# A state-space stage cut into short steps between projection blocks, with half of one map and the table loads moved to GpSimd

## The chip, the cores and the metric

The kernel runs on one core of one Trainium2 chip. The metric is the device time of one execution in microseconds (us), the median of the runs shown. Matrix products run on TensorE (PE, its weight loads PEld), elementwise work on VectorE (DVE), ScalarE (ACT) and GpSimd (POOL). SyncE (SP) issues DMAs; GpSimd can issue them too. Each engine takes its instructions in order, and a wait on one holds everything behind it on that engine.

## The reference

Two layers on a sequence of 512 tokens with 1024 channels, in float32; each is `x <- x + RMSNorm_post(mixer(RMSNorm_pre(x)))`. The change touches layer 0, whose mixer has two branches:

```
p = u @ ev_w_in[j]                       # 1024 -> 5120
a_in, a_z, b_val, b_gate, b_z = split(p)
ya = s5_layer(a_in, ...)                 # 64 groups of 16 channels, 64 complex states each
ya = gelu(ya)
ya = ya * sigmoid(ya @ s5_w_glu + s5_b_glu) * silu(a_z)
yb = conformer_conv(b_val, b_gate, ...)  # GLU, depthwise conv of 31 taps, LayerNorm, swish, projection
y  = concatenate([ya, yb * silu(b_z)]) @ ev_w_out
```

The state-space layer computes `s_t = Lbar s_(t-1) + Bbar u_t` and `y_t = Re(C s_t) + D u_t` per group. Layer 1 is a gated linear attention, which the change leaves as it is.

## The kernel before, in words

**Projections.** Every float32 product is made of three passes: a weight is split into a high part `wh` and a low part `wl` (float32r), the activation into `uh` and `ul`, and `mm_st` (L181) adds `wh uh`, `wh ul` (L186, L187) and `wl uh` (L189) into one PSUM bank. One block is 24 such matmuls on 512 columns and makes 128 output channels. Layer 0 has 40 input blocks: eight `a` blocks (the state-space input), and eight each of value `v`, gate `g`, `zb` and `za`. `wlist` (L85 to L94) holds the order of their weights: all `a` first, then v, g, zb, za for each j.

**Weights.** `w_raw` (L113) loads a block's 512 KB by SyncE's queue into `wraw`, which has three buffers. `w_low` (L122) makes the low part: ScalarE writes the negated rounding (L130), and a DMA that GpSimd issues adds the raw weights to it (L131). ScalarE also makes `wh` (L143). A raw buffer is free when all this has read it. `w_get` keeps one block split ahead.

**The state-space stage** works on eight chunks of eight groups. `s5_params` (L308) computes tables on VectorE and GpSimd: powers `pr` (nine of them, real and imaginary) and `prb`, and the phase tables' factors `wb`. `s5_prep(c)` (L513) loads a chunk's B and C matrices `cb` by SyncE's queue (L519); makes `cr_` (C's real part with a sign per half, L522) and `ci_` (its negated imaginary part, L523) on ScalarE; and, per half of four groups: the input map `bmt`, three products with `outer` (L528, L530, L532) on VectorE for the first two chunks and on GpSimd after; its transposes (L544) into `bm`; the response (L551), copied to `ks` (L554), transposed (L555), and written to `kt` (L557); the output map `cme`, three products on VectorE. Then `kt` goes through DRAM into the Toeplitz matrix `tm` (L563, L565). For every other chunk `phases` (L492) builds two tables `ph0`, `ph1` on GpSimd in six products, which four DMAs on SyncE's queue duplicate into `ct` and `st` (L573). `s5_in` (L579) loads `u` back from DRAM (L584), applies `bm` (L588), turns the result (L595), rotates, scans and rotates back on VectorE and ScalarE. `s5_out` (L619) applies `tm` and `cme` (L628) and transposes to channels with a GELU (L637, L643).

**The convolution** (`conv`, L649): 30 VectorE multiply-adds of 745 ns for each of eight channel blocks (L655, L656), marked `background`.

**What sets the order.** The generators `s5_prep`, `s5_in` and `s5_out` yield between their steps, and a loop (L703) writes the steps of chunks c, c+1 and c+2, then four blocks. This written order is a priority. The scheduler that builds the program places each engine's instructions by priority among those that its own timing says are ready; `feed()` raises a priority by 1500 places and `background()` lowers it by 4000. A pool opened with `reuse_waits="tile"` waits for the earlier owners of its bytes tile by tile.

Of the kernel before, what the change touches and what calls it, by code (L numbers as in the profile page):

```python
# [51 lines left out]
def trunk(ctx: ExitStack, tc: tile.TileContext, A: dict, out: bass.AP, dbg: dict | None = None):  # L52
# [33 lines left out]
    for j in range(8):  # L86
        wlist.append(A["w_in0"][j])
    for j in range(8):
        wlist.append(A["w_in0"][16 + j])
        wlist.append(A["w_in0"][24 + j])  # L90
        wlist.append(A["w_in0"][32 + j])
        wlist.append(A["w_in0"][8 + j])
# [20 lines left out]
    def w_raw():  # L113
        i = wst["next_raw"]
        if i >= len(wlist):
            return
        raw = wpool.tile([P, 1024], F32, tag="wraw", bufs=3, name=f"wraw{i}")
        SY.dma_start(raw, wlist[i])
        wst["raw"][i] = raw
        wst["next_raw"] = i + 1  # L120
# [187 lines left out]
    def s5_params():  # L308
# [148 lines left out]

        G.memset(md, 0.0)
# [6 lines left out]
    q5 = S5.enter_context(tc.tile_pool(name="q5", bufs=1, side="right", reuse_waits="tile"))  # L465
    h5 = S5.enter_context(tc.tile_pool(name="h5", bufs=2, side="right", reuse_waits="tile"))
# [25 lines left out]
    def phases(c):  # L492
# [10 lines left out]
        out_ = []  # L503
        for o, (a, b, op) in enumerate(((0, 1, ALU.subtract), (1, 0, ALU.add))):
            r_ = h5.tile(sh, F32, tag=f"ph{o}", bufs=1, name=f"ph{o}_{c}")
            wt = h5.tile(sh, F32, tag="wt", bufs=1, name=f"wt{o}_{c}")
            G.tensor_tensor(out=r_, in0=w1(0), in1=w0(a), op=ALU.mult)
            G.tensor_tensor(out=wt, in0=w1(1), in1=w0(b), op=ALU.mult)
            G.tensor_tensor(out=r_, in0=r_, in1=wt, op=op)
            out_.append(r_.rearrange("p g a b -> p (g a b)"))  # L510
        pair[c // 2] = out_

    def s5_prep(c):  # L513
# [3 lines left out]
        gs = slice(g0_, g0_ + GC)  # L517
        cb = h5.tile([P, 4, GC, GP], F32, tag="cb", bufs=2, name=f"cb{c}")
        SY.dma_start(cb, A["s5cb"][c])  # L519
# [3 lines left out]
        SC.mul(ci_, cb[:, 1], -1.0)  # L523
# [10 lines left out]
        bm = q5.tile([P, GC, P], F32, tag="bm", bufs=2, name=f"bm{c}")  # L534
        cme = q5.tile([P, GC, TB, GP], F32, tag="cme", bufs=3, name=f"cme{c}")
        kt = q5.tile([P, GC, GP], F32, tag="kt", bufs=2, name=f"kt{c}")
        for h in range(2):
            hs = slice(h * 4, h * 4 + 4)
            bmt = q5.tile([P, 4, GP, TB], F32, tag="bmt", bufs=2, name=f"bmt{c}")
            pt1 = h5.tile([P, 4, GP, TB], F32, tag="wt", bufs=1, name=f"pt1_{c}")  # L540
            outer(pe_, bmt, pt1, h, prb, cb[:, 2, hs], cb[:, 3, hs], 2)
            tp = ps("aux")
            for j in range(4):
                PE.transpose(tp[:, j * P:(j + 1) * P], bmt[:, j].rearrange("p q s -> p (q s)"), ident)  # L544
            with feed():
                SC.copy(bm[:, hs, :], tp.rearrange("p (g n) -> p g n", n=P))
            yield

            kp = ps("aux")
            for j in range(4):  # L550
                PE.matmul(kp[32 * j:32 * j + 32, 0:P], cr_[:, h * 4 + j, :], bmt[:, j].rearrange("p q s -> p (q s)"), start=True, stop=True)  # L551
# [3 lines left out]
            PE.transpose(kp[:, P:2 * P], ks, ident)  # L555
            with feed():
                V.tensor_tensor(out=kt[:, hs, :], in0=kp[:, P:2 * P].rearrange("p (g q) -> p g q", q=32)[:, :, 0:GP],  # L557
                                in1=dg[:, g0_ + h * 4:g0_ + h * 4 + 4, :], op=ALU.add)
            pt2 = q5.tile([P, 4, TB, GP], F32, tag="pt", bufs=1, name=f"pt2_{c}")
            outer(V, cme[:, hs], pt2, h, pr, cr_[:, hs, 0:GP], ci_[:, hs], 3)  # L560
            yield
# [4 lines left out]

        if c % 2 == 0:
            phases(c)
        half = slice(c % 2 * NS, c % 2 * NS + NS)
        ct_, st_ = (h5.tile([P, S], F32, tag=n, bufs=2, name=f"{n}{c}") for n in ("ct", "st"))  # L570
        for dst, src in zip((ct_, st_), pair[c // 2]):
            for r_ in range(2):
                SY.dma_start(dst[r_ * NS:r_ * NS + NS], src[half])  # L573
        prep[c] = (bm, cme, tm, ct_, st_)
        yield

    state = {}

    def s5_in(c):  # L579

        g0_ = c * GC
        bm, cme, tm, cc, ss = prep.pop(c)
        u = h5.tile([P, GC, NB], F32, tag="u", name=f"u{c}")
        SY.dma_start(u, bass.AP(tensor=u_d[c].tensor, offset=u_d[c].offset, ap=[[NB, P], [S * GP, GC], [1, NB]]))  # L584
        gp = ps("aux")
# [73 lines left out]
    for c in range(KT):  # L659
# [3 lines left out]
        with feed():  # L663
            ai = tmp((P, TB, NB))
            SC.copy(ai, acc.rearrange("p (b s) -> p s b", s=TB))
            SY.dma_start(u_d[c], ai)

    def value_gate(c):
        w = w_get()
        av = ps()  # L670
        mm_st(av, w, uh, ul)
        w = w_get()
        ag = ps()
        mm_st(ag, w, uh, ul)
        h = hpool.tile([P, 30 + S], F32, tag="h", name=f"h{c}")
        G.memset(h[:, 0:30], 0.0)
        with feed():
            sg = tmp()
            SC.activation(sg, ag, AF.Sigmoid)  # L679
            V.tensor_mul(h[:, 30:30 + S], av, sg)  # L680
        htile[c] = h
        with background():
# [534 lines left out]
```

## Time and profile before

| | |
|---|---|
| median of 3 runs | 944.95 us (944.75 to 949.93) |
| the profiled execution | 946.38 us, span 944.7 us |
| mean granted TensorE clock | 0.981 |
| ScalarE, VectorE, GpSimd busy | 485.1, 641.9, 245.4 us |
| HBM read, written | 95.18 MB, 13.22 MB |
| low-part DMAs (L131) | 56, median 6.1 us from issue to landing |
| input weight loads | 40, median 5.2 us from issue to landing |

A row of waits names the instruction that waited, after the arrow what released it, then the total, the number of times and the longest, in us. A row of a timeline gives the start, the duration, the engine, the line, the operation and its shape, and in brackets the idle time before it with what ended it. A row of grouped lines gives count, busy time, mean ns of one, and the idle time before. A row of windows gives the stretch, its length, each engine's busy time (PE, PEld, DVE, ACT, POOL; with an engine filter that engine alone), the granted clock, the DMA engines' mean busy share, and GB/s. SPq rows are DMA issues; their duration includes SyncE's wait before them. Matmuls overlap, so one's duration is longer than the distance between two starts.

### The profile page before, as it was taken

The numbers are of one execution on the slowest core, as the hardware profiler recorded it, in microseconds if no ns is written. First come the engines' busy times: TensorE is split into PE (matmuls) and PEld (weight loads), VectorE is DVE, ScalarE is ACT, GpSimd is POOL, SyncE is SP. The second block draws the span as 40 slices with busy tenths as digits, with TensorE's granted clock in tenths as the row PEclk, the third lists the DMA queues.
The fourth block names the chain that finished last, engine by engine and source line by source line (L and its number), as shares of the span: only waits on it lengthen the run. The fifth ranks groups of instructions, "written<-read, shape, count | busy, mean of one in ns | idle before, by whom it ended". The sixth has DMA issues, their size and how long they took to land. (4 is left out here: it accounts for less than half of the span.)

```text
span 944.7 us, 12134 instructions
## 1 busy us (share of the span) xinstructions
PE 897.7 (95%) x4396; PEld 718.9 (76%) x4396; DVE 641.9 (68%) x1206; ACT 485.1 (51%) x693; POOL 245.4 (26%) x258
## 2 busy tenths in 40 slices
PE   5995998999999999999999979999999999999996
PEld 4873776777778877778887758888888888888875
DVE  7953999999989989832579477584483232744546
ACT  6542786786678855564444566343543242523430
POOL 2693657463123422011054002000200020000222
PEclk8998999999999999999999979999999999999998
DMA  9877987787988885288463112212212223324412
GB/s 278 228 198 194 229 199 184 178 205 204 215 220 228 210 231 179 92 224 201 153 215 124 45 63 93 84 37 82 90 67 90 73 83 135 134 89 164 193 45 89
DMA packets 54955, 142.74 MB, mean 151 GB/s; under 512 B 14256, under 2 KB 15792, under 8 KB 54896
## 3 DMA queue, kind: packets, MB, share of 16 engines
q1 hardware_dynamic: 46832, 112.62, 35.9%
q0 software_dynamic: 8064, 29.36, 17.3%
q8 instruction: 34, 0.56, 0.2%
q14 instruction: 25, 0.20, 0.1%
HBM read 95.18 MB, written 13.22 MB: 115 GB/s over the span
## 5 line engine op out<-in xcount | busy, mean ns | idle before, releaser
L143 ACT CAST wh<-wraw 128x1024 fp32r<-128x1024 f32 x126 | 132.1, 1048 | 161.4 <-PE ps_mm L801 92.5
L149 DVE TENSOR_TENSOR wl<-wraw,wh 128x1024 fp32r<-128x1024 f32 x70 | 87.0, 1243 | 115.2 <-ACT wh L143 114.8
L655 DVE SCALAR_TENSOR_TENSOR ps_cv<-h,cw,ps_cv 128x512 f32<-128x512 f32 x232 | 161.7, 745 | 2.7 <-ACT ps_cv L652 1.8
L186 PE MATMUL ps_mm<-u0h,wh 128*128 128x512 f32 x320 | 129.9, 407 | 1.0 <-ACT tmp L679 0.7
L187 PE MATMUL ps_mm<-u0l,wh 128*128 128x512 f32 x320 | 129.4, 405 | 0.0
L800 PE MATMUL ps_mm<-wh,u1h 128*128 128x512 f32 x240 | 96.2, 402 | 3.5 <-ACT wh L143 3.4
L801 PE MATMUL ps_mm<-wh,u1l 128*128 128x512 f32 x240 | 96.3, 401 | 0.8 <-DVE u1l L194 0.8
L131 POOL DMA_DIRECT2D wl<-wraw x56 | 48.9, 884 | 182.4 <-ACT wl L130 178.2
L802 PE MATMUL ps_mm<-wl,u1h 128*128 128x512 f32 x240 | 91.6, 401 | 1.6 <-DVE wl L149 1.6
L189 PE MATMUL ps_mm<-u0h,wl 128*128 128x512 f32 x320 | 82.5, 395 | 1.1 <-DMA wl<-wraw 1.1
L186 PEld LDWEIGHTS ps_mm<-u0h,wh 128*128 128x128 f32 x320 | 61.8, 193 | 16.4 <-issue 1.6
L130 ACT ACTIVATE wl<-wraw 128x1024 fp32r<-128x1024 f32 x56 | 59.2, 1057 | 25.8 <-DMA wraw<-in_w_in_dram 14.0
L187 PEld LDWEIGHTS ps_mm<-u0l,wh 128*128 128x128 f32 x320 | 61.7, 193 | 13.9 <-issue 1.1
L189 PEld LDWEIGHTS ps_mm<-u0h,wl 128*128 128x128 f32 x320 | 59.4, 188 | 14.9 <-DMA wl<-wraw 1.5
L800 PEld LDWEIGHTS ps_mm<-wh,u1h 128*128 128x128 f32 x240 | 45.9, 191 | 14.9 <-ACT wh L143 3.8
L971 POOL TENSOR_TENSOR rg<-rg,ng 128x512 f32<-128x512 f32 x16 | 24.2, 1544 | 124.6 <-ACT rg L970 124.6
L802 PEld LDWEIGHTS ps_mm<-wl,u1h 128*128 128x128 f32 x240 | 45.6, 191 | 13.1 <-DVE wl L149 2.3
L801 PEld LDWEIGHTS ps_mm<-wh,u1l 128*128 128x128 f32 x240 | 45.9, 191 | 11.7 <-DVE u1l L194 1.2
L186 PE MATMUL ps_mm<-u1h,wh 128*128 128x512 f32 x128 | 50.7, 396 | 0.0
L187 PE MATMUL ps_mm<-u1l,wh 128*128 128x512 f32 x128 | 50.5, 394 | 0.0
L1062 POOL TENSOR_TENSOR kr<-kr,fac 128x384 f32<-128x384 f32 x8 | 6.7, 837 | 124.2 <-DVE rr L205 65.1
L800 PE MATMUL ps_mm<-wh,oth 128*128 128x512 f32 x96 | 37.8, 396 | 0.5 <-ACT wh L143 0.5
(341 smaller groups left out, 1993.6 us busy)
## 6 DMA issues: line engine op xcount, KB each, us to landing
wl<-wraw POOLq DMA_DIRECT2D x56, 512.0 KB, 6.1
wraw<-in_w_in_dram SPq DMA_DIRECT2D x40, 512.0 KB, 5.2
wraw<-in_w_out_dram SPq DMA_DIRECT2D x32, 512.0 KB, 3.3
wraw<-in_w_vr_dram SPq DMA_DIRECT2D x32, 512.0 KB, 3.2
wraw<-in_w_qk_dram SPq DMA_DIRECT2D x16, 512.0 KB, 3.3
tm<-kt_d SPq DMA_DIRECT2D x8, 512.0 KB, 6.3
wraw<-in_w_glu_dram SPq DMA_DIRECT2D x8, 512.0 KB, 5.8
wraw<-in_w_pw_dram SPq DMA_DIRECT2D x8, 512.0 KB, 5.1
```

Of the source, the lines that this page charges most:

```text
L130: SC.activation(l, raw, AF.Copy, scale=-1.0)
L131: G.dma_start(l.bitcast(F32), raw, accum_op=ALU.add)
L143: SC.copy(h, raw)
L149: V.tensor_tensor(out=l, in0=raw, in1=h.bitcast(F32), op=ALU.subtract)
L186: PE.matmul(acc, whv[:, k, :], xh[:, k, :], start=(k == 0), stop=False)
L187: PE.matmul(acc, whv[:, k, :], xl[:, k, :], start=False, stop=False)
L189: PE.matmul(acc, wlv[:, k, :], xh[:, k, :], start=False, stop=(k == KT - 1))
L655: V.scalar_tensor_tensor(out=acc, in0=h[:, k:k + S], scalar=cw[:, c, k:k + 1], in1=acc, op0=ALU.mult, op1=ALU.add)
L800: PE.matmul(accs[tt], xh[:, kt, ts_], whj, start=(first and j == 0), stop=False)
L801: PE.matmul(accs[tt], xl[:, kt, ts_], whj, start=False, stop=False)
L802: PE.matmul(accs[tt], xh[:, kt, ts_], wlj, start=False, stop=(last and j == 1))
L971: G.tensor_tensor(out=r_, in0=r_, in1=ng, op=ALU.mult)
```

## The change

- The blocks are written in another order: a0, a1, v0, g0, a2 to a7, zb0, za0, and then v, g, zb, za for j from 1. `block` replaces the separate loops.
- `s5_prep` has six short steps instead of five; `turn`, `response`, `turn_response` and `output_map` are functions, and the turned response has a PSUM buffer of its own. `s5_in` has three steps, the load of `u` alone being the first. Sixteen blocks are written around the first chunks' steps, and 2, 2, 2, 3, 3, 4, 4, 4 blocks in the eight turns of the loop.
- The second half's output map is made on GpSimd for chunks 2 to 7.
- `cb` is loaded by GpSimd's queue. The two phase tables are one tile, and two DMAs of GpSimd's queue a chunk copy it into `cs`, in place of four of SyncE's.
- The signs of C go into `pr` once, in `s5_params` after `prb` is made; `ci_` is gone, and the output map reads `cb` itself. `cr_` stays for the response.
- Every fourth raw weight of the first 36 goes into a buffer in the pool `q5`; `cme` has two buffers instead of three.
- The parameters `par` are loaded after the second x tile instead of after the first weight.

```diff
+    order0 = [("a", 0), ("a", 1), ("v", 0), ("g", 0)] + [("a", j) for j in range(2, 8)] + [("zb", 0), ("za", 0)]
+    for j in range(1, 8):
+        order0 += [("v", j), ("g", j), ("zb", j), ("za", j)]
...
-        raw = wpool.tile([P, 1024], F32, tag="wraw", bufs=3, name=f"wraw{i}")
+        if i < 36 and i % 4 == 3:
+            raw = wst["pool"].tile([P, 1024], F32, tag="wraw", bufs=1, name=f"wraw{i}")
+        else:
+            raw = wpool.tile([P, 1024], F32, tag="wraw", bufs=3, name=f"wraw{i}")
...
         SY.dma_start(x_t[tt], A["x"][tt * P:(tt + 1) * P, :])
+        if tt == 1:
+            SY.dma_start(par, A["s5p"])
...
+        V.tensor_scalar(out=pr[:, 0], in0=pr[:, 0], scalar1=sgn, scalar2=None, op0=ALU.mult)
+        V.tensor_scalar(out=pr[:, 1], in0=pr[:, 1], scalar1=-1.0, scalar2=None, op0=ALU.mult)
...
-        SY.dma_start(cb, A["s5cb"][c])
-        cr_ = csps[c % 2]
-        ci_ = h5.tile([P, GC, GP], F32, tag="ci", bufs=1, name=f"ci{c}")
-        SC.activation(cr_[:, :, 0:GP], cb[:, 0], AF.Copy, scale=sgn)
-        SC.mul(ci_, cb[:, 1], -1.0)
+        G.dma_start(cb, A["s5cb"][c])
...
+        def turn_response(h, ks):
+            kp = ps("aux")
+            PE.transpose(kp[:, 0:P], ks, ident)
+            with feed():
+                V.tensor_tensor(out=kt[:, hs[h], :], in0=kp[:, 0:P].rearrange("p (g q) -> p g q", q=32)[:, :, 0:GP],
+                                in1=dg[:, g0_ + h * 4:g0_ + h * 4 + 4, :], op=ALU.add)
...
+        def output_map(h):
+            eng = G if h and c >= DVE_PREP else V
...
+            outer(eng, cme[:, hs[h]], pt2, h, pr, cb[:, 0, hs[h]], cb[:, 1, hs[h]], 3)
+
+        input_map(0)
+        yield
+        bm = q5.tile([P, GC, P], F32, tag="bm", bufs=2, name=f"bm{c}")
+        cr_ = csps[c % 2]
+        turn(0)
+        SC.activation(cr_[:, :, 0:GP], cb[:, 0], AF.Copy, scale=sgn)
+        yield
+        cme = q5.tile([P, GC, TB, GP], F32, tag="cme", bufs=2, name=f"cme{c}")
+        kt = q5.tile([P, GC, GP], F32, tag="kt", bufs=2, name=f"kt{c}")
+        ks = response(0)
+        input_map(1)
+        output_map(0)
+        yield
+        turn_response(0, ks)
+        turn(1)
+        if c % 2 == 0:
+            phases(c)
+        yield
+        ks = response(1)
+        output_map(1)
+        half = slice(c % 2 * NS, c % 2 * NS + NS)
+        cs = h5.tile([P, 2, S], F32, tag="cs", bufs=2, name=f"cs{c}")
+        for r_ in range(2):
+            G.dma_start(cs[r_ * NS:r_ * NS + NS], pair[c // 2][half])
+        prep[c] = (bm, cme, cs[:, 0], cs[:, 1])
+        yield
+        turn_response(1, ks)
...
+    blocks(6)
+    run(P_[0])
+    blocks()
+    run(P_[0])
+    blocks()
+    run(P_[0])
+    blocks()
+    run(P_[0], P_[1], I_[0])
+    blocks()
+    run(P_[0], P_[1])
+    blocks()
+    run(P_[0], I_[0], P_[1])
+    blocks()
+    run(I_[0], P_[1])
+    blocks(2)
+    run(P_[1], P_[2], I_[1])
+    blocks(2)
     for c in range(KT):
...
+        n = (2, 2, 2, 3, 3, 4, 4, 4)[c]
+        run(O_[c], nx, p1, p2)
+        blocks(n - n // 2 - n // 3)
+        run(nx, p2, O_[c])
+        blocks(n // 3)
+        run(p2)
+        blocks(n // 2)
+        run(p2, p3)
+        if c + 2 < KT:
+            run(I_[c + 2])
```

More of the change, by code (lines that the diff above doesn't have):

```diff
@@ L85, in trunk @@
     wlist = []
[L86 to L92, printed above, removed]
+    order0 = [("a", 0), ("a", 1), ("v", 0), ("g", 0)] + [("a", j) for j in range(2, 8)] + [("zb", 0), ("za", 0)]
+    for j in range(1, 8):
+        order0 += [("v", j), ("g", j), ("zb", j), ("za", j)]
+    for n, j in order0:
+        wlist.append(A["w_in0"][{"a": 0, "za": 8, "v": 16, "g": 24, "zb": 32}[n] + j])
     for j in range(8):
@@ L565, in s5_prep @@
         SY.dma_start(tm, bass.AP(tensor=kd.tensor, offset=kd.offset, ap=[[(2 * TB - 1) * P, GP], [P, TB], [1, TB * P]]))
[L567 to L574, printed above, removed]
+        tms[c] = tm
         yield
+    tms = {}
     state = {}
@@ L656, in conv, with block @@
         V.scalar_tensor_tensor(out=h[:, 30:30 + S], in0=h[:, 30:30 + S], scalar=cw[:, c, 30:31], in1=acc, op0=ALU.mult, op1=ALU.add)
-    for c in range(KT):
+    half_glu = {}
+    def block(n, c):
         w = w_get()
@@ L662, in trunk @@
         mm_st(acc, w, uh, ul)
[L663 to L682, printed above, removed]
-            conv(c)
@@ L685, in trunk @@
[L685 to L716 removed]
+        if n == "a":
+            with feed():
+                ai = tmp((P, TB, NB))
+                SC.copy(ai, acc.rearrange("p (b s) -> p s b", s=TB))
+                SY.dma_start(u_d[c], ai)
+        elif n == "v":
+            half_glu[c] = acc
+        elif n == "g":
+            h = hpool.tile([P, 30 + S], F32, tag="h", name=f"h{c}")
+            G.memset(h[:, 0:30], 0.0)
+            with feed():
+                sg = tmp()
+                SC.activation(sg, acc, AF.Sigmoid)
+                V.tensor_mul(h[:, 30:30 + S], half_glu.pop(c), sg)
+            htile[c] = h
+            with background():
+                conv(c)
+        else:
+            with feed():
+                sg = tmp()
+                SC.activation(sg, acc, AF.Silu)
+                SY.dma_start((za_d if n == "za" else zb_d)[c], sg)
@@ new lines, in trunk, with blocks, run @@
+    za_d, zb_d = ([dram.tile([P, S], F32, name=f"z{n}_d{c}") for c in range(KT)] for n in "ab")
+    todo = iter(order0)
+    def blocks(n=1):
+        for _ in range(n):
+            b = next(todo, None)
+            if b:
+                block(*b)
+    def run(*gs):
+        for g in gs:
+            next(g, None)
+    P_ = [s5_prep(c) for c in range(KT)]
+    I_ = [s5_in(c) for c in range(KT)]
+    O_ = [s5_out(c) for c in range(KT)]
+    none = iter(())
+    blocks(6)
+    run(P_[0])
+    blocks()
```

77 lines of the change are left out of this document (25 added, 52 removed).

## The prediction

> **What bounds the kernel now.** I read the page first, then TensorE's waits, then the four queues around its longest wait, then what is late behind it. The profiled execution took 946.38 us, 1.43 over the median of 944.95; the sum is made against it and the 1.43 comes off at the end. About 1% (9.4 us) either way is what a measurement here can tell from no change.
>
> ```profile
> span 944.7 us, 12134 instructions
> PE 897.7 (95%) x4396; PEld 718.9 (76%) x4396; DVE 641.9 (68%) x1206; ACT 485.1 (51%) x693; POOL 245.4 (26%) x258
> ```
>
> TensorE is the bound: almost every gain must be a hole in its stream. TensorE's waits are these (total, times, longest):
>
> ```profile
> PE ps_aux L555 <- ACT ks L554: 10.4, 1, 10.4
> PE ps_mm L300 <- DVE x L297: 10.3, 3, 7.8
> PE ps_aux L551 <- DVE kt L557: 4.2, 3, 1.8
> PE ps_aux L588 <- DMA u<-u_d: 1.7, 1, 1.7
> PE ps_mm L189 <- DMA wl<-wraw: 1.1, 1, 1.1
> PE ps_aux L544 <- ACT ya L643: 0.9, 1, 0.9
> PE ps_mm L186 <- ACT tmp L679: 0.7, 1, 0.7
> ```
>
> All but the second lie in the stage that the change rewrites. The first is a single hole. Here are its rows in the timelines of TensorE, ScalarE and SyncE's DMA queue:
>
> ```profile
> 92.74 0.48 PE L555 MATMUL ps_aux<-ident,ks 128*128 128x128 f32 x1 [10.38 <-ACT ks L554]
> ```
> ```profile
> 91.28 0.31 ACT L523 ACTIVATE ci<-cb 128x128 f32<-128x128 f32 x1 [8.99 <-DMA cb<-in_s5cb_dram]
> 91.49 1.03 ACT L143 CAST wh<-wraw 128x1024 fp32r<-128x1024 f32 x1
> 92.43 0.26 ACT L554 COPY ks<-ps_aux 128x128 f32<-128x128 f32 x1
> ```
> ```profile
> 69.82 5.10 SPq L573 DMA_DIRECT2D st<-ph  x4
> 75.64 10.08 SPq L118 DMA_DIRECT2D wraw<-in_w_in_dram  x3
> 85.81 0.58 SPq L519 DMA_DIRECT2D cb<-in_s5cb_dram  x1
> ```
>
> Read backwards: L555 transposes `ks`; ScalarE copies `ks` only after `ci` (L523); `ci` waits 8.99 us for the table `cb`; SyncE issues `cb` at 85.81, behind three weight loads over which it sat 10.08 us for free raw buffers, behind the phase-table loads (the last four, st, held its queue for 5.10). Nobody was short of arithmetic; three in-order queues stood behind one another.
>
> **The change, part by part.**
>
> *Tables by GpSimd's queue, `ci` gone, fourth raw buffer: the stall.* `ci` disappears, because its sign goes into `pr` once; the load of `cb` no longer stands behind weight loads; a fourth raw buffer means that SyncE blocks less at L118; sixteen `cs` loads on GpSimd replace 32 ct/st loads on SyncE. The whole 10.4 us should go. What is late next? The `wh` at 91.49 stood only behind `ci` (its row names no wait of its own), so no second hole stands right behind. After the hole TensorE ran at half pace:
>
> ```profile
> 94.74 0.63 PE L187 MATMUL ps_mm<-u0l,wh 128*128 128x512 f32 x1
> 95.16 0.63 PE L186 MATMUL ps_mm<-u0h,wh 128*128 128x512 f32 x1
> 100.14 0.39 PE L186 MATMUL ps_mm<-u0h,wh 128*128 128x512 f32 x1
> 100.36 0.39 PE L187 MATMUL ps_mm<-u0l,wh 128*128 128x512 f32 x1
> 70.80:94.50 23.70, 13.32 (x73) 9.07 (x72) 7.21 (x12) 5.41 (x10) 8.61 (x8) 0.82 0.78 195
> ```
>
> Starts are 0.42 apart instead of 0.22, and the granted clock of that slice is 0.82. The 3 us from 92.74 to about 95.7 would take half: 1.5. Together -11.9; bounds: 0 (the hole comes back elsewhere) to -11.9.
>
> *Short steps.* Each half's transposes, response and turned response become separate steps with projection blocks between, and the turned response gets a PSUM buffer of its own. The wait L551 <- kt is for an `aux` buffer that VectorE has yet to empty; with no ScalarE hop inside one buffer's life, I take 3.0 of its 4.2. `u` is loaded a step ahead: 1.4 of 1.7. The fourth raw buffer takes the 1.1 at L189. The `ya` and `tmp` waits (0.9, 0.7) I leave. Together -5.5, bounds 0 and -8.6.
>
> *Reordered blocks and start.* The same 40 blocks run; one costs 5.49 us, by the starts of two successive low-part groups:
>
> ```profile
> 33.57 1.99 PE L189 MATMUL ps_mm<-u0h,wl 128*128 128x512 f32 x8
> 39.06 1.99 PE L189 MATMUL ps_mm<-u0h,wl 128*128 128x512 f32 x8
> 0.00:23.60 23.60, 13.12 (x53) 10.66 (x54) 17.82 (x75) 15.75 (x23) 6.77 (x27) 0.86 0.95 278
> 16.98 0.79 PE L186 MATMUL ps_mm<-u0h,wh 128*128 128x512 f32 x1 [0.23 <-DVE u0l L305]
> 36.88 0.52 DVE L401 TENSOR_TENSOR pr<-s5u,s5u 128x256 f32<-128x256 f32 x1
> ```
>
> DMA is at 0.95 in the first slice, at 278 GB/s. The 96 KB of `par` ahead of two x tiles cost 0.35 us, and two `cb` tables of 256 KB, which GpSimd's queue may now issue ahead of everything, up to 1.9: +2.2 at worst, nothing at best, since the tables are issued at the start now too, only behind x. A gain is excluded: x comes no sooner. I take +0.7. The two multiplications that sign `pr` lie on VectorE in its parameter chain; six blocks cover TensorE from 17 until 17 + 6 x 5.49 = 50 us, and `pr` is done at 37.4, so they cost nothing; without that cover they would cost two operations on 576 elements, about 1 by the 0.52 for 256.
>
> *Half the output map on GpSimd.* Six chunks, three operations each, and 24 more DMA issues (8 cb, 16 cs). The rows of GpSimd and VectorE:
>
> ```profile
> 60.00:330.00 270.00, 124.16 (x110) 0.97 0.83 205
> L131 POOL DMA_DIRECT2D wl<-wraw x35 | 30.3, 867 | 95.9 <-ACT wl L130 91.7 <-PE ps_mm L187 2.9 <-PE ps_mm L189 1.3
> L532 POOL TENSOR_TENSOR bmt<-bmt,pt 128x512 f32<-128x512 f32 x12 | 17.6, 1464 | 0.8
> L528 POOL TENSOR_TENSOR bmt<-prb,cb 128x512 f32<-128x512 f32 x12 | 17.1, 1423 | 10.2 <-PE ps_aux L551 10.2
> L530 POOL TENSOR_TENSOR pt<-prb,cb 128x512 f32<-128x512 f32 x12 | 15.5, 1289 | 0.9
> L532 DVE TENSOR_TENSOR cme<-cme,pt 128x512 f32<-128x512 f32 x16 | 14.0, 877 | 0.1
> ```
>
> GpSimd gets 6 x (1.464 + 1.423 + 1.289) = 25.1 us and 24 x 0.867 = 20.8: from 124 to 170 us of that stretch, two thirds. VectorE loses 18 x 0.88 = 16 us, and conv(0), ready after block 4 instead of block 10, can fill its two long idle times before 92 us (10.17 and 14.03):
>
> ```profile
> 68.92 0.69 DVE L530 TENSOR_TENSOR pt<-prb,cb 128x512 f32<-128x512 f32 x1 [10.17 <-POOL ph L509]
> 91.62 0.69 DVE L530 TENSOR_TENSOR pt<-pr,ci 128x512 f32<-128x512 f32 x1 [14.03 <-ACT ci L523]
> 75.45 1.37 POOL L507 TENSOR_TENSOR ph<-wb 128x512 f32<-128x512 f32 x1 [5.75 <-DMA ct<-ph]
> ```
>
> The danger is GpSimd's order: every low part of a weight is issued by it (L131), and `cb` and `cs` now too, each behind what waits. One chunk costs GpSimd two input halves 8.35, an output half 4.18, half of the six products of a phase table (the same shape) 4.18, three table loads 2.60 and two low parts 1.73: 21.0. TensorE's chunk, while only two blocks stand between (the first three chunks), is at least 10.98. So GpSimd is short up to 10 a chunk, 30 in three, unless it works ahead. By the row at 75.45 it is free at about 70 us, and chunk 2 is due after 16 blocks, near 17 + 16 x 5.49 = 105 at the earliest: a lead of 35, less 12.5 for one chunk's maps, covers 22.5 and leaves 7.5. TensorE's own small matmuls lengthen its chunk and cover more. It can't go below nothing, as what it frees on VectorE is counted with the short steps. Upper bound, with no lead and the waits at L131 (95.9 / 35 = 2.7 each, two a chunk) in full: (21.0 + 5.4 - 11) x 3 = 46. I take a third of the 7.5, +2.5, near the lower end, since none of TensorE's waits above is for GpSimd.
>
> GpSimd also slows VectorE where both run:
>
> ```profile
> 149.98 1.75 DVE L611 TENSOR_TENSOR zb<-zb,ct 128x512 f32<-128x512 f32 x1
> 176.96 0.68 DVE L611 TENSOR_TENSOR zb<-zb,ct 128x512 f32<-128x512 f32 x1
> 149.59 1.60 POOL L509 TENSOR_TENSOR ph<-ph,wt 128x512 f32<-128x512 f32 x1
> ```
>
> The operation takes 1.75 beside a GpSimd product, 0.68 alone: 1.07 more. Eighteen new GpSimd operations could give back 18 x 1.07 = 19 of the 16 that VectorE saves. The Trainium skill, "SBUF — State Buffer", section "SBUF: two separate sides", says that the two engines' shared port pair is an exclusive lock held for a whole instruction; by it this transfer of work would be worth nothing or less to VectorE, and these rows agree. The same section warns that a VectorE operation in a 2-port mode can hold up the descriptors of a DMA issued by GpSimd; no row here isolates that.
>
> Late behind the stage is VectorE's convolution and LayerNorm, due when TensorE asks for `xbh`:
>
> ```profile
> 396.84 0.68 DVE L194 TENSOR_TENSOR xbl<-ln,xbh 128x512 fp32r<-128x512 f32 x1
> 413.00 0.47 PE L186 MATMUL ps_mm<-xbh,wh 128*128 128x512 f32 x1 [0.88 <-ACT wh L143]
> ```
>
> It has 413 - 397 = 16 us of slack, which a TensorE 14 us earlier nearly uses up; the earlier conv(0) refills it.
>
> **The sum.** 946.4 - 11.9 - 5.5 + 0.7 + 2.5 = 932.2; less 1.4 for the median: **930.8**, 1.5% faster. With the other bounds of the small terms (start 0 to 2.2, short steps 3 to 8.6, GpSimd 0 to 7.5), not all at once, this case spans 925 to 938.
>
> **The rivals.**
>
> *The hole moves.* SyncE's 10.08 at L118 and the DMA share of 0.78 to 0.95 speak for weights as the next thing late: `wl` must be loaded, subtracted and accumulated within a block's 5.49. Against it: L189 waited 1.1 in the whole trace, and a buffer is added. Also, the written order is only a priority: the scheduler lays out each engine's queue by its own estimates when the kernel is built, so the steps may stand otherwise than written. It returns about 11: 942.
>
> *VectorE blocked.* The port rows above, at their full 19, with TensorE waiting for kt, za and h as VectorE falls behind: a net loss of 3, the 5.5 of the short steps not gained: 930.8 + 8.5 = 939.3. Against it: VectorE's 24 us of idle time above.
>
> *GpSimd becomes the choke (the other side).* Its in-order queue holds the low weights while it waits or multiplies; it decides once chunk 2's maps are begun later than about 105 us. Price: the lead gone, the 30 in place of 2.5: 930.8 - 2.5 + 30 = 958.3. For it: 95.9 us of waits at L131. Against: its start at 70 us, and that TensorE can run later blocks meanwhile.
>
> *More than forecast.* GpSimd and the start cost nothing, and all of the 8.6 goes: 930.8 - 2.5 - 0.7 - 3.1 = 924.5. What speaks for it: the holes named are all of TensorE's waits in the stage. Against it: two of them (ya, tmp) the change does not touch.
>
> **How the numbers follow.** Forecast 0.52, the hole moves 0.18, VectorE blocked 0.07, choke 0.10, more 0.13. Faster by over 1% (under 935.5): nearly all of the forecast (0.49), all of the last, a little of the middle two (0.02): 0.64. Slower by over 1% (over 954.4): 0.09 of the choke's 0.10. The rest, 0.27, is the same. The range, 920 to 946, takes in all but the choke and the tails of the others.
>
> **What would show it.** Right: no wait of TensorE over 3 us between 20 and 330 us; no `cb` wait on ScalarE; clock 1.0 there; GpSimd near 290 us in all and VectorE's cme at 10 operations of each kind in place of 16; first L186 between 16 and 19 us. Wrong: L189 waiting for wl by several us (the hole moved), L544 or L628 waiting for GpSimd (the choke), VectorE products near 1.5 us throughout (the lock), or the S5 stage ending no earlier than now.

## The result, and the profile after

The changed kernel takes 956.62 us (median of 4 runs, 955.28 to 957.88) beside 944.85 us for the kernel before (now four runs): a ratio of 1.0112, 95% interval 1.0081 to 1.0144. Forecast was 930.8 us, with a range of 920 to 946. The change makes the kernel slower, by 11.8 us between the medians and 10.6 by the ratio, instead of faster by 14.

The head of the page and TensorE's waits of the profiled execution (956.0 us; line, after the arrow the releaser, total us, times, longest):

```profile
span 954.2 us, 12084 instructions
PE 900.9 (94%) x4396; PEld 723.3 (76%) x4396; DVE 649.0 (68%) x1190; ACT 484.5 (51%) x685; POOL 275.4 (29%) x300
```
```profile
PE ps_mm L304 <- DVE x L301: 11.5, 4, 7.9
PE ps_aux L660 <- DVE kt L565: 6.8, 2, 3.8
PE ps_mm L189 <- ACT wh L146: 6.4, 2, 5.5
PE ps_mm L192 <- DMA wl<-wraw: 5.7, 2, 4.9
...
PE ps_aux L563 <- ACT ks L558: 1.5, 1, 1.5
PE ps_mm L189 <- DVE u0l L309: 1.4, 1, 1.4
```

The edited lines moved: L186, L187, L189 are now L189, L190, L192; L131 is L134; L554 is L558; L557 is L565. The 10.4 us for `ks` (1.5 are left) and ScalarE's wait for `cb` are gone, as forecast. In their place stand 6.4 for `wh` and 5.7 for `wl`, which was 1.1, and the wait for `kt` has grown from 4.2 to 6.8. GpSimd has 30 us more work, as worked out (25 from the products). VectorE is the surprise: it lost 18 products, and is busy 7.1 us longer.

All of the loss lies ahead of w_glu. Its first matmul, in the kernel before and in the changed one:

```profile
320.10 0.40 PE L186 MATMUL ps_mm<-yah,wh 128*128 128x512 f32 x1
```
```profile
329.38 0.39 PE L189 MATMUL ps_mm<-yah,wh 128*128 128x512 f32 x1
```

It comes 9.3 us later, and from there to the end of the span both need the same 624.6 and 624.8 us. Three places make up the loss.

**The start.** The first projection matmul came at 16.98; now (TensorE, ScalarE, GpSimd):

```profile
20.70 0.79 PE L189 MATMUL ps_mm<-u0h,wh 128*128 128x512 f32 x1 [1.36 <-DVE u0l L309]
```
```profile
8.87 1.06 ACT L221 ACTIVATE junk<-x 128x1024 bf16<-128x1024 f32 x1 [2.00 <-DMA x<-in_x_dram]
```
```profile
2.13 1.29 POOL L524 DMA_DIRECT2D cb<-in_s5cb_dram  x2
```

GpSimd issues the two tables at 2.13 us, among the x loads; ScalarE waits 2.00 us for the third x tile and reaches the fourth at 10.46 instead of 8.37, 2.1 us late. The rest of the 3.7 us comes on VectorE. With `par` loaded earlier, its small parameter operations start at 6.15 instead of 12.25 and stand between the steps that lead to `u0l`: ScalarE's first `u0h` is 2.6 us late (17.88 instead of 15.30), VectorE's first `u0l` 3.7. Before and after:

```profile
16.18 0.74 DVE L305 SCALAR_TENSOR_TENSOR u0l<-ps_mm,vec,u0h 128x512 fp32r<-128x512 f32 x1
```
```profile
19.89 0.75 DVE L309 SCALAR_TENSOR_TENSOR u0l<-ps_mm,vec,u0h 128x512 fp32r<-128x512 f32 x1
```

**The fourth weight.** SyncE's queue, and what TensorE, ScalarE and GpSimd made of it:

```profile
6.22 24.87 SPq L121 DMA_DIRECT2D wraw<-in_w_in_dram  x4
...
37.48 0.78 SPq L121 DMA_DIRECT2D wraw<-in_w_in_dram  x1
```
```profile
36.98 1.99 PE L192 MATMUL ps_mm<-u0h,wl 128*128 128x512 f32 x8
...
44.46 0.79 PE L189 MATMUL ps_mm<-u0h,wh 128*128 128x512 f32 x1 [5.49 <-ACT wh L146]
...
57.80 3.78 PE L192 MATMUL ps_mm<-u0h,wl 128*128 128x512 f32 x8 [4.93 <-DMA wl<-wraw]
```
```profile
42.42 1.06 ACT L133 ACTIVATE wl<-wraw 128x1024 fp32r<-128x1024 f32 x1 [7.22 <-DMA wraw<-in_w_in_dram]
```
```profile
53.20 0.88 POOL L134 DMA_DIRECT2D wl<-wraw  x1
```

Counted from 0, the four loads at 6.22 are those of blocks 2, 4, 5 and 6; the one at 37.48 is block 3, the first load into the new buffer. It is issued behind three blocks that are needed after it. ScalarE stands 7.22 us for it, TensorE 5.49; then GpSimd, busy with small products, issues the low part only at 53.20, 9.7 us after ScalarE has written its part, and TensorE waits again. From the third block's low part to the fourth's are 20.8 us instead of 5.5. The second and third slice of the windows (length, then busy time of PE, PEld, DVE, ACT, POOL, then clock, DMA share, GB/s) show the price: 11.4 us of TensorE's time missing (5.49 and 5.92), the clock at 0.87 and 0.84, and the DMA engines at a share of 0.49 and 0.70.

```profile
23.60:47.20 23.60, 18.11 (x74) 14.40 (x73) 23.45 (x62) 8.10 (x11) 17.90 (x39) 0.87 0.49 134
47.20:70.80 23.60, 17.68 (x69) 13.11 (x68) 19.89 (x19) 6.91 (x10) 21.36 (x24) 0.84 0.70 163
```

**Late holes for kt.** Around 205 us, on TensorE, VectorE, GpSimd and TensorE again:

```profile
195.71 0.27 PE L563 MATMUL ps_aux<-ident,ks 128*128 128x128 f32 x1
```
```profile
197.69 4.13 DVE L638 TENSOR_TENSOR za<-za,zb 128x512 f32<-128x512 f32 x1
...
205.50 0.21 DVE L565 TENSOR_TENSOR kt<-ps_aux,dg 128x64 f32<-128x64 f32 x1
```
```profile
197.60 1.39 POOL L531 TENSOR_TENSOR pt<-prb,cb 128x512 f32<-128x512 f32 x1
198.63 1.38 POOL L529 TENSOR_TENSOR bmt<-prb,cb 128x512 f32<-128x512 f32 x1
199.67 1.60 POOL L533 TENSOR_TENSOR bmt<-bmt,pt 128x512 f32<-128x512 f32 x1
```
```profile
205.76 0.69 PE L660 MATMUL ps_aux<-tm,u 128*64 128x128 f32 x4 [3.04 <-DVE kt L565]
```

A VectorE product that takes 0.68 us elsewhere takes 4.13: it starts 0.09 after the first of three GpSimd products and ends 0.55 after the third. TensorE has turned the response by 196 us, but `kt` is written only at 205.50, because it stands in VectorE's queue behind that product, the scan and multiply-adds of the convolution. Without the 3.45 us more, by an estimate from these rows, `kt` would be done at about 202.3, before TensorE falls idle at 202.7. The other wait for `kt`, 3.8 us at 260.31, has two such products ahead of it (3.21 and 2.26 us).

### The profile page after: what moved, and what is told of

It reads as the page before. It is cut to its first block, busy times and chain, and to the rows that moved or that the text cites. A ratio compares the mean times of both kernels' runs of the same rounds, so it can differ in the third digit from the quotient of the medians.

```text
span 954.2 us, 12084 instructions
## 1 busy us (share of the span) xinstructions
PE 900.9 (94%) x4396; PEld 723.3 (76%) x4396; DVE 649.0 (68%) x1190; ACT 484.5 (51%) x685; POOL 275.4 (29%) x300
## 5 line engine op out<-in xcount | busy, mean ns | idle before, releaser
L687 DVE SCALAR_TENSOR_TENSOR ps_cv<-h,cw,ps_cv 128x512 f32<-128x512 f32 x232 | 169.3, 751 | 5.1 <-ACT ps_cv L684 1.7
L189 PE MATMUL ps_mm<-u0h,wh 128*128 128x512 f32 x320 | 130.4, 408 | 6.9 <-ACT wh L146 5.5
L190 PE MATMUL ps_mm<-u0l,wh 128*128 128x512 f32 x320 | 128.0, 400 | 0.0
L134 POOL DMA_DIRECT2D wl<-wraw x56 | 51.8, 932 | 137.8 <-ACT wl L133 108.4
L192 PE MATMUL ps_mm<-u0h,wl 128*128 128x512 f32 x320 | 84.1, 402 | 5.7 <-DMA wl<-wraw 5.7
L189 PEld LDWEIGHTS ps_mm<-u0h,wh 128*128 128x128 f32 x320 | 61.8, 193 | 23.1 <-ACT wh L146 5.9
L192 PEld LDWEIGHTS ps_mm<-u0h,wl 128*128 128x128 f32 x320 | 60.4, 192 | 19.8 <-DMA wl<-wraw 6.5
L190 PEld LDWEIGHTS ps_mm<-u0l,wh 128*128 128x128 f32 x320 | 61.6, 193 | 13.1 <-issue 0.6
L189 PE MATMUL ps_mm<-u1h,wh 128*128 128x512 f32 x128 | 50.7, 396 | 0.0
L190 PE MATMUL ps_mm<-u1l,wh 128*128 128x512 f32 x128 | 50.5, 394 | 0.0
```

The costliest lines, as they stand in the source:

```text
L134: G.dma_start(l.bitcast(F32), raw, accum_op=ALU.add)
L189: PE.matmul(acc, whv[:, k, :], xh[:, k, :], start=(k == 0), stop=False)
L190: PE.matmul(acc, whv[:, k, :], xl[:, k, :], start=False, stop=False)
L192: PE.matmul(acc, wlv[:, k, :], xh[:, k, :], start=False, stop=(k == KT - 1))
L687: V.scalar_tensor_tensor(out=acc, in0=h[:, k:k + S], scalar=cw[:, c, k:k + 1], in1=acc, op0=ALU.mult, op1=ALU.add)
```

## The experiments

My theory had three parts. A: the first load into the new buffer is late, because the pool `q5` takes the place of start-up buffers and opens only when they are closed. B: tables and parameters crowd the x loads. C: rows of GpSimd products hold VectorE, so the move of half the output map costs time. (The chain to `kt` that I gave with e3 runs through the scan and ScalarE. ScalarE does stand 7.67 us for the scan, but `ks` was copied before that, at 191.07; in the rows above it is VectorE's own queue that makes `kt` late.) The rivals: DMA and GpSimd are simply over-asked (D), VectorE's load is what decides (F). All kernels were timed in five rounds against the kernel before, whose median was 946.0 to 946.8 us in these groups; the ratios are to be compared. In kernels with the start undone, line numbers from 290 on are lower by one.

| kernel | median us | ratio to before | 95% interval |
|---|---|---|---|
| changed kernel | 956.62 | 1.0112 | 1.0081 to 1.0144 |
| e1: load 3 in the ring | 943.01 | 0.9965 | 0.9953 to 0.9977 |
| e2: start as before | 954.35 | 1.0096 | 1.0083 to 1.0109 |
| e3: output map on VectorE | 960.98 | 1.0144 | 1.0118 to 1.0171 |
| e4: all three | 941.30 | 0.9942 | 0.9919 to 0.9966 |
| e5: no extra buffer | 946.35 | 0.9999 | 0.9978 to 1.0020 |
| e6: e1 and e2 | 937.24 | 0.9903 | 0.9883 to 0.9923 |
| e8: e6, whole output map on GpSimd | 935.33 | 0.9884 | 0.9863 to 0.9904 |
| e9: e6, cs by SyncE | 941.75 | 0.9951 | 0.9928 to 0.9973 |
| f2: before, tables by GpSimd | 940.03 | 0.9930 | 0.9909 to 0.9951 |
| f3: f2 and signed powers | 937.93 | 0.9906 | 0.9886 to 0.9925 |
| g1: extra buffer in h5 | 942.70 | 0.9951 | 0.9933 to 0.9969 |
| g3: e8 with g1's buffer | 933.87 | 0.9856 | 0.9830 to 0.9882 |
| o1: e6, old order of blocks | 929.95 | 0.9824 | 0.9806 to 0.9843 |
| o2: e6, even spacing | 942.02 | 0.9957 | 0.9942 to 0.9971 |
| o3: e6, early chunks wide | 952.97 | 1.0071 | 1.0054 to 1.0087 |
| o4: g3, even spacing | 943.04 | 0.9952 | 0.9934 to 0.9971 |
| p1: o1 with g1's buffer | 930.86 | 0.9838 | 0.9819 to 0.9857 |
| p2: p1, whole output map on GpSimd | 936.78 | 0.9899 | 0.9876 to 0.9921 |

### The late load: e1, g1, e5

```diff
-        if i < 36 and i % 4 == 3:
+        if 3 < i < 36 and i % 4 == 3:
```

> The changed kernel, with the fourth weight block's load (raw 3) put back into the old ring of three buffers; every later fourth load (7, 11, ... 35) stays in the extra buffer. Theory A: the extra buffer's first load was issued at 37.48 us, behind loads 4 to 6, because its pool opens only after the start-up pools close; ScalarE's low part, the 5.49 us wait at L189, the 4.93 us wait at L192 and the half clock after both hang on that one load. Then raw 3 is issued by about 20 us, the two waits go, and the time falls by 9 to 15 us, to 942 to 948 us. Rival D: from 20 to 60 us the DMA engines and GpSimd's queue are simply over-asked by the new steps, and some weight block is late whichever buffer it uses: then a wait for wl or wh of another block of 4 to 10 us stands between 40 and 65 us, and the time stays within 4 us of 956.6.

One load moved brings 1.47% (13.9 us of 945), as theory A said. TensorE's waits of e1 for weights, and its second and third slice:

```profile
PE ps_mm L192 <- DMA wl<-wraw: 4.6, 4, 2.4
...
PE ps_mm L189 <- ACT wh L146: 0.9, 1, 0.9
```
```profile
23.60:47.20 23.60, 23.60 (x104) 19.30 (x104) 23.45 (x60) 11.56 (x16) 17.86 (x38) 1.00 0.74 180
47.20:70.80 23.60, 19.61 (x86) 15.15 (x85) 23.56 (x27) 10.62 (x13) 23.05 (x29) 1.00 0.84 212
```

TensorE is busy without a gap from 23.6 to 47.2, at full clock, with more on the DMA engines and the same load on GpSimd. So D is out. That it is the place in `q5` and not the buffer as such, g1 shows: the extra buffer stays, for load 3 too, but in `h5`.

```diff
-    wst["pool"] = q5
     h5 = S5.enter_context(tc.tile_pool(name="h5", bufs=2, side="right", reuse_waits="tile"))
+    wst["pool"] = h5
```

> The changed kernel with one edit: the extra weight buffer is a tile of the pool h5 (where the tables lie) instead of q5; all else as changed, load 3 and every fourth after it go there. Theory A': it is only the pool that delays the first load; q5's place is taken by start-up buffers until about 36 us, h5's is free from the start. Then load 3 is issued by about 20 us, the waits of 5.5 and 4.9 us at L189 and L192 are gone, and the time is that of the kernel with load 3 in the ring (943.0 us) or a little less, 939 to 943.5, as loads 4 to 6 come one block earlier. Rival: an early fourth load only crowds the input loads and tables (DMA at 0.9 and more in the first 24 us); then a wait for wl or wh of 3 us or more stays, and the time is 946 to 953.

Its interval overlaps that of e1. SyncE's queue now has five loads in one row, and the two waits of 5.49 and 4.93 us are gone:

```profile
7.01 24.98 SPq L121 DMA_DIRECT2D wraw<-in_w_in_dram  x5
```

One part of theory A is only argued: `q5` and `h5` are opened on neighbouring lines, behind the same closed pools, so the difference must be whose bytes the buffer takes, and no run shows which start-up buffer that was. Nor did SyncE wait for those bytes at 37.48: its list has no wait there, the scheduler had placed the load so late.

What the later loads into the buffer are worth:

```diff
-        if i < 36 and i % 4 == 3:
+        if i < 0:
```

> The changed kernel without the extra weight buffer: all loads of layer 0 use the ring of three, as before; everything else as changed. It tells what loads 7 to 35 in the extra buffer are worth, against the kernel with only load 3 put back (943.0 us). Theory A (only the first load of the extra buffer did harm; a fourth buffer is worth about the 1.1 us that TensorE waited for wl before): 943 to 946 us. Rival D, that weights are late under the new order whichever buffer they use: without the fourth buffer they are later still, 948 us or more, with TensorE's waits at L192 for wl over 8 us in all (4.6 with load 3 put back). If the extra buffer is no use at all: 943 us or less, with L192's waits no longer than 4.6.

Against e1, 0.34% (3.2 us) slower, the intervals just apart; L192 waited 2.4 in all, so the gain is not in that row, and where it lies is open.

### The start: e2

```diff
-        G.dma_start(cb, A["s5cb"][c])
+        (SY if c < 2 else G).dma_start(cb, A["s5cb"][c])
...
-        if tt == 1:
-            SY.dma_start(par, A["s5p"])
     SY.dma_start(vec, A["vec"])
     w_raw()
+    SY.dma_start(par, A["s5p"])
```

> The changed kernel, with the tables (cb) of chunks 0 and 1 loaded by SyncE's queue again (GpSimd's queue from chunk 2 on), and the parameter load back behind the first weight load, as before. Theory B: the first projection matmul came at 20.70 us instead of 16.98 because these three transfers stand among the four input loads; then it comes at 17 to 18 us, and the time falls by 2.5 to 4 us, to 952.5 to 954 us. Rival E: the start is late because VectorE's parameter arithmetic now starts earlier and lies between its u0l products; as the parameter load is moved back too, this kernel does not tell the two apart by its time, but its rows do: the wait of ScalarE's L221 for x (2.00 us in the changed kernel) gone means B, u0l at L308 spread with foreign products between means E. If the start is hidden later (the late weight load sets the pace anyway), the time stays within 1 us of 956.6.

```profile
17.31 0.79 PE L189 MATMUL ps_mm<-u0h,wh 128*128 128x512 f32 x1 [0.23 <-DVE u0l L308]
```

The first matmul is back by 3.4 us, but the time fell by only 0.16%, which the intervals do not separate: TensorE only reaches the late fourth block sooner. With that block on time (e6 against e1) the same edit brings 0.62%, 5.9 us; where the 2.5 us beyond the first matmul come from is open. In e2 the first `u0l` follows the first `u0h` by 0.89 us, as before the change (0.88; 2.01 in the changed kernel), but e2 moves tables and parameters back together, so no run prices them apart.

### The output map: e3, e4, e6, e8

```diff
-            eng = G if h and c >= DVE_PREP else V
+            eng = V
```

> The changed kernel, with both halves of the output map on VectorE for every chunk, and none on GpSimd. Theory C: three GpSimd products in a row (1.4 us each) hold VectorE's next instruction until the row ends (4.13 us for a product of 0.68 us), the scan comes late, ScalarE stands 7.6 us behind it, and TensorE waits 3.0 and 3.8 us for kt near 205 and 260 us. Then those rows go: the late waits at L660 for kt fall from 6.8 us in all to under 2, and the time falls by 4 to 10 us, to 947 to 953 us, although VectorE has about 16 us more work. Rival F: VectorE's own load decides there, as it was what the move was meant to relieve; then VectorE's products of the state-space steps queue behind 16 us more work and the time rises by 0 to 6 us, to 957 to 963 us.

> The changed kernel with the three undone together: raw 3 in the ring, tables of chunks 0 and 1 and the parameters loaded as before, the output map on VectorE. What is left of the change is the order of blocks and steps, the signed powers, the tables of chunks 2 to 7 by GpSimd's queue, one phase copy per half and the later extra buffers. Theories A, B and C add up: 9 to 15, 2.5 to 4 and 4 to 10 us less than 956.6, with some overlap 930 to 940 us, below the kernel before by 5 to 15 us. If the order itself costs time (rival G), it stays at or above 945 us though all three are undone.

Theory C fell in its conclusion here. The waits for `kt` did fall from 6.8 to 1.2 us, but the time did not: e3 is no faster than the changed kernel, and e4 (12 runs between 934.66 and 945.72, the traced one the longest) is little better than e1, with overlapping intervals. TensorE's new waits in e3:

```profile
PE ps_aux L660 <- DVE sv L647: 4.5, 3, 3.7
PE ps_mm L189 <- ACT yah L196: 2.2, 1, 2.2
...
PE ps_aux L660 <- DVE kt L565: 1.2, 1, 1.2
```

VectorE, with 18 products more, delivers `sv` late, and at the end of the stage holds ScalarE for 3.30 us, where `wh` is queued further behind (ScalarE and TensorE of e3):

```profile
323.10 0.78 ACT L684 ACTIVATE ps_cv<-h,vec,cw 128x512 f32<-128x512 f32 x1 [3.30 <-DVE h L710]
```
```profile
335.26 0.79 PE L189 MATMUL ps_mm<-yah,wh 128*128 128x512 f32 x1 [4.32 <-ACT wh L146]
```

> The changed kernel with load 3 back in the ring, and the tables of chunks 0 and 1 and the parameters loaded as before; GpSimd keeps its half of the output map. The two gains measured apart were 13.6 and 2.3 us. Added up: 940 to 941.5 us; with some overlap up to 943. Against the kernel that has the output map on VectorE as well (941.3 us, spread 934.7 to 945.7): theory F (VectorE's load decides, the move to GpSimd is worth 4 us, as the kernel with only that undone said) gives 937 to 941 us; theory C (the rows of GpSimd products cost more than they save) gives 942 to 948.

> As the kernel with load 3 in the ring and the start as before, but with both halves of the output map on GpSimd from chunk 2 on: 18 more products there (about 25 us) and 18 fewer on VectorE (about 16 us). It doubles the move. Theory F (VectorE's load decides): a further 2 to 5 us less than with one half moved. Theory C (rows of GpSimd products hold VectorE, and GpSimd's queue gets late): holes at L660 for kt grow from 6.7 us to 10 or more, GpSimd's low parts of the weights (L134) come late, and the time rises by 5 to 20 us.

e6 against e4 prices the move of one half alone: 0.39% (3.7 us) for it, with intervals that just overlap. The second half brings 0.19% more, which the intervals do not separate; it does not cost 5 to 20 us. All of this points to F, that VectorE's load decides, but each of these steps lies inside the intervals or at their edge, and in the old order of blocks the second half costs 0.61% (p2 against p1 below, intervals apart). So neither C nor F is shown as a rule. The holding is real all the same. VectorE's busy time went from 656.8 (e3) to 649.0 (changed kernel): 7.8 us for 18 products that cost 15.8 at the 877 ns of the row before. Half of the saving is given back in longer VectorE instructions, on balance: the groups below became longer, others shorter (L647 fell from 1253 to 702 ns). Groups of VectorE's lines in e3, then in the changed kernel (busy us, mean ns):

```profile
L531 DVE TENSOR_TENSOR pt<-pr,cb 128x512 f32<-128x512 f32 x16 | 16.9, 1055 | 4.1 <-DMA cb<-in_s5cb_dram 4.0
...
L638 DVE TENSOR_TENSOR za<-za,zb 128x512 f32<-128x512 f32 x8 | 7.6, 950 | 0.0
L637 DVE TENSOR_TENSOR zb<-zb,cs 128x512 f32<-128x512 f32 x8 | 6.8, 846 | 0.0
```
```profile
L531 DVE TENSOR_TENSOR pt<-pr,cb 128x512 f32<-128x512 f32 x10 | 15.1, 1505 | 3.3 <-DMA cb<-in_s5cb_dram 3.2
...
L637 DVE TENSOR_TENSOR zb<-zb,cs 128x512 f32<-128x512 f32 x8 | 10.3, 1288 | 0.0
L638 DVE TENSOR_TENSOR za<-za,zb 128x512 f32<-128x512 f32 x8 | 9.3, 1169 | 0.0
```

### The hole of the kernel before: f2, f3

f2 is the kernel before with `(G if c >= 2 else SY).dma_start(cb, ...)`; f3 is f2 with the two multiplications of `pr` added and `ci_` removed.

> The kernel before with one edit: the tables (cb) of chunks 2 to 7 by GpSimd's queue; ci, the order of the steps, the blocks, the three weight buffers and the output map stay as before. The prediction says that TensorE's wait of 10.4 us for ks, and the 1.5 us of half clock behind it, come from the place of cb's load in SyncE's queue. If so, they go with this edit alone: 933 to 937 us against 944.9. If the hole only moves to the next thing that is late in SyncE's queue (the rival that I gave 942), it stays at 940 to 946, with a wait of 5 us or more for weights, tm or kt near 80 to 110 us.

The tables alone brought 0.70%. A hole of 4.3 us stayed, and ScalarE shows why: `ci` still waits, because GpSimd's queue issues the table at 82.01, behind phase products that wait for SyncE's phase loads (ScalarE, then GpSimd).

```profile
85.60 0.31 ACT L523 ACTIVATE ci<-cb 128x128 f32<-128x128 f32 x1 [6.51 <-DMA cb<-in_s5cb_dram]
85.81 1.03 ACT L143 CAST wh<-wraw 128x1024 fp32r<-128x1024 f32 x1
86.75 0.26 ACT L554 COPY ks<-ps_aux 128x128 f32<-128x128 f32 x1
```
```profile
82.01 0.60 POOL L519 DMA_DIRECT2D cb<-in_s5cb_dram  x1
```

> The kernel before with the tables of chunks 2 to 7 by GpSimd's queue, and the signed powers (no ci). With the tables alone it was 940.0 us: a hole of 4.3 us was left for ks, as ScalarE still stood 6.51 us at ci for a table that GpSimd's queue issued at 82 us. If ci is what was left of the hole, this one falls to 934 to 938 us with no wait for ks over 1 us. If another instruction takes the place of ci (csp needs the same table), it stays at 939 to 942.

Without `ci` no wait for `ks` is left in TensorE's list, and the two edits together bring 0.94%, 8.9 us (0.75% to 1.14%); f2 and f3 by themselves are not separated by their intervals. This small part of the change brings most of what the whole was forecast to bring.

### Phase loads back on SyncE: e9

e9 is e6 with `SY.dma_start(cs[...` for `G.dma_start(cs[...`.

> The changed kernel with load 3 in the ring and the start as before (937.2 us), but with the 16 phase loads (cs) issued by SyncE's queue instead of GpSimd's. It prices that part of the move: GpSimd saves 9 us of issuing and 14 us of standing at L595 for a free cs buffer, SyncE's queue gets the wait instead, with weight loads behind it. If GpSimd's queue was the costly place: 932 to 936 us. If SyncE's is, as it was in the kernel before: 938 to 945, with waits for wh or wl growing from 4.3 us in all. I hold the second for a little likelier.

0.48% slower than e6, and TensorE waits for weights.

```profile
PE ps_mm L192 <- DMA wl<-wraw: 7.2, 3, 5.2
```

The longest of these waits, 5.2 us at 93.94, comes by way of GpSimd: SyncE issues the second pair of cs loads at 77.12, behind a weight load and a store (in e6 GpSimd issues all four at 70.19). GpSimd stands 15.92 us, 6.55 in e6, before the next phase product, which overwrites the table that they read, and issues low parts of weights only from 88.73 on. That this product waited for the cs loads is read from the code; the trace names another DMA. So with this layout moving the loads to GpSimd was right, though GpSimd stands 14.0 us in front of them (GpSimd's group in the changed kernel):

```profile
L596 POOL DMA_DIRECT2D cs<-ph x16 | 9.2, 652 | 14.0 <-DVE zc L644 14.0
```

### Order and spacing: g3, o1 to o4, p1, p2

f3 (0.9906) has the hole mended and nothing else. e4 (0.9942) has that too, and in addition the new order, the short steps, the cs loads on GpSimd and the later extra buffers. These together brought nothing; 3.4 us more are the difference, with intervals that overlap a little. The last runs ask what in them costs.

> All that the runs so far point to: the changed kernel with the extra buffer in the early pool h5, the tables of chunks 0 and 1 and the parameters loaded as before, and both halves of the output map on GpSimd from chunk 2. The same with load 3 in the ring took 935.3 us. The early fourth buffer should bring up to 4 us more, as the waits at L192 near 65 to 81 us (3.2 us in all) are for weight blocks: 931 to 936 us. If it crowds the start instead: 936 to 940.

o1 writes all `a` blocks first, then v, g, zb, za; o2 sets `n = 3`, o3 `n = (4, 4, 4, 3, 3, 2, 2, 2)[c]`, in place of `(2, 2, 2, 3, 3, 4, 4, 4)[c]`.

> The changed kernel with load 3 in the ring and the start as before (937.2 us), with the 40 blocks in the order of the kernel before (eight u blocks first, then value, gate and the two z blocks of each chunk); the steps and their spacing stay. It prices the two early blocks v0 and g0. If they matter (conv(0) starts four blocks earlier and fills VectorE's idle time, as the prediction said), the time rises by 2 to 6 us, to 939 to 943. If the early blocks do harm, it falls by as much. If the order of blocks is of no weight: 936 to 938.5.

> As the kernel of 937.2 us, with three projection blocks after every chunk's steps instead of 2, 2, 2, 3, 3, 4, 4, 4. Theory H (the first three chunks stand too close for VectorE and GpSimd): the holes between 160 and 262 us (7.7 us in the two lists at L659 for kt and sv) shrink by half and the time falls by 2 to 5 us, to 932 to 935. If the load of all chunks together decides, and not their spacing, the holes only move to later chunks: 936 to 939.

> As the kernel of 937.2 us, with 4, 4, 4, 3, 3, 2, 2, 2 blocks after the chunks. Theory H: the holes at 160 to 262 us vanish; but the last chunks stand close and little is left to cover them before w_glu begins, so that a hole for sv or for the last ya of 2 to 8 us comes at 290 to 320 us: 932 to 940, and less than the even spacing only if the tail is covered. If spacing has no weight: 936 to 939.

> The fastest kernel so far (extra buffer in h5, start as before, both halves of the output map on GpSimd: 933.9 us) with three blocks after every chunk. Theory H: 929 to 932. If GpSimd's products are what set the chunk's length there, no gain: 933 to 936.

Theory H fell: the wider the early chunks, the slower. In o3 the tail is bare:

```profile
312.93 0.69 PE L659 MATMUL ps_aux<-cme,sv 128*64 128x128 f32 x4 [9.34 <-DVE sv L646]
...
322.87 1.22 PE L189 MATMUL ps_mm<-yah,wh 128*128 128x512 f32 x2 [4.29 <-ACT yah L196]
```

The changed spacing is the best of the three: it leaves blocks where the last chunks need cover. The old order of blocks, however, is 0.79% (7.5 us) better in o1. TensorE's waits for `kt`, in e6 and in o1:

```profile
PE ps_aux L659 <- DVE kt L564: 6.1, 2, 3.8
```
```profile
PE ps_aux L659 <- DVE kt L564: 0.4, 1, 0.4
```

Not all of it is gained: o1 waits 3.8 us for `za` in their place, e6 0.6.

> The kernel of 930.0 us (old order of blocks, start as before, load 3 in the ring, half the output map on GpSimd), with the extra buffer in h5 from load 3 on. The pool alone changed the time by 0.3 us with the new order. If the old order is worth 7 us whatever the layout: 928 to 931.5. If 930.0 was one lucky layout of the queues: 933 to 938.

> The same with both halves of the output map on GpSimd from chunk 2; with the new order of blocks it took 933.9 us. If the old order is worth 7 us whatever the layout: 925 to 929. If it was one lucky layout: 932 to 937.

p1 keeps the gain, p2 does not: with the whole output map on GpSimd the old order (p2, 0.9899) is slower than the new one (g3, 0.9856), the intervals just overlapping. So value and gate early are not worth a fixed number of us either way, and neither is the second half of the output map. Every such edit makes the scheduler lay out all queues anew, and kernels with the same work in another order differ by up to 7.5 us. Which row of o1's layout makes the difference stays open; the `kt` waits are only where it shows. The same holds for the other steps of 3 to 6 us above (GpSimd's half, the cs loads, the later extra buffers): each is what the edit did in this surrounding, and its worth by itself is not settled. The late load is better founded: its two waits are in the rows, TensorE's starts are about twice as far apart for some 3.5 us after each, and by the first w_glu matmul the changed kernel is 12.4 us behind e1 (329.38 and 317.00). So are the 3.4 us at the first matmul.

The fastest kernel here is o1: 929.95 us, 1.76% under the kernel before (1.57% to 1.94%), p1 beside it.

## Why the prediction was wrong

**The failed step** is "the fourth raw buffer takes the 1.1 at L189", and before it "a fourth raw buffer means that SyncE blocks less at L118". I priced the buffer as one more place and never asked from when on the place exists. Its first load is the fourth block's, in `q5` that load comes behind three later ones, and 13.9 us hang on that (e1, g1). The premise did not hold for the later loads either: up to 330 us SyncE's waits in front of weight loads add up to 148 us before, 178 in the changed kernel and 179 without the extra buffer (e5), so SyncE did not block less. Without the late load the range would have held, but not the forecast: e1 is at 943.0.

**The stall, -11.9.** Right in mechanism, too large: -8.9 (f3), and within its bounds. From 20 to 330 us TensorE's waits add up to 19.0 us before and 10.2 in f3: the 10.4 are gone, but those for `u`, `wl` and `bmt` grew by 3.7. f2's rows show that the tables' queue alone was not enough to close the hole, and f3's that it closes without `ci`.

**Short steps, -5.5.** Did not come. From f3 to e4, where they lie together with the new order, the cs loads and the later extra buffers, the time rises by 3.4 us. In e4's list the wait for `kt` did shrink (4.2 to 1.5) and that for `u` is gone, but `wl` grew from 1.1 to 3.7, and new waits appeared, 4.3 for `wh` and 3.7 for `sv`. Which of the four parts costs is open.

**The start, +0.7, bounds 0 and 2.2.** 3.7 at the first matmul, 5.9 in the time once nothing hides it (e6 against e1). I costed the bytes of the transfers, 0.35 and 1.9 us, and the fourth x tile is indeed 2.1 us late. The other 1.6 at the first matmul are parameter operations that VectorE puts ahead of the x tiles and `u0l` once `par` comes early; I had no term for them.

**GpSimd's load, +2.5, bounds 0 and 46.** Its sign came out the other way: half the output map on GpSimd is worth -3.7 (e6 against e4, at the edge of the noise). I had excluded a gain with the argument that VectorE's relief was counted elsewhere. I had also let VectorE give back up to all that it saves; it gives back half.

**The rivals.** The choke named 958.3; that this is close to the time is chance. It was to decide at chunk 2, near 105 us, through GpSimd's load, and the loss came earlier and went with one load (e1); more load on GpSimd did no harm in e8, though it cost 5.8 us in p2. One piece of it is in the trace, the low part issued at 53.20 behind other products; that piece vanished with the late load. "The hole moves" came nearest in kind, weights as the next thing late, at 30 to 60 us instead of 85, and for a reason that I had not seen. Of the marks, the wait for wl by several us (now L192), named for a wrong forecast, was met, and the first matmul missed the 16 to 19 us named for a right one.

In order, each by its ratio: tables and signed powers bring 8.9 us; order, steps, cs loads and later extra buffers take back 3.4; GpSimd's half brings 3.7; the start costs 5.9; the late load 13.9. That ends at +10.6, the measured ratio, as it must: each step is the difference of two kernels in one chain (f3, e4, e6, e1, changed), and in another order the steps would have other sizes. Against the forecast of -14 the late load makes 13.9 of the difference, the short steps with what lies beside them 8.9, the start 5.2 and the stall 3.0; GpSimd's half takes off 6.2.

## What to carry to other kernels

A new buffer is worth something only from the moment at which its bytes are free: before counting on it, ask which load uses it first, when that load is due, and who owned the place till then. A change in several parts should be taken apart, as here two small edits carried a gain of 0.9% that one late load of 512 KB and three early transfers more than ate up. And where several in-order queues are nearly full, moving a step is priced by running it, because the layout around it changes by as much as the step is worth.

## What was not expected of the hardware

A VectorE product beside one GpSimd product took 1.75 us in the kernel before; here one took 4.13 us, through three GpSimd products in a row, with no turn for VectorE between them. Near 250 us two more, of 3.59 and 3.21 us, end like it 0.55 us after the last product of such a row. The Trainium skill, "SBUF — State Buffer", section "SBUF: two separate sides", has the lock held for one whole instruction. These rows fit a lock that GpSimd takes again before VectorE gets it. Still VectorE keeps half of the saving in busy time. And the late load cost more than its two waits: 13.9 us, where the waits are 10.4. The granted clock of the two slices is 0.87 and 0.84, and after each wait eight matmuls start 0.43 to 0.45 us apart, where 0.23 is usual in this trace; that is 3.4 us more. That 10.4 and 3.4 make up the 13.9 so closely is partly luck, as e1 has 4.0 us of TensorE's time missing in the second slice itself.
